# An mLSTM and pooling block on one core: decay rows behind the first queries, squares on VectorE, later casts, stores on SyncE

## The chip, the core and the metric

The kernel runs on one core of a Trainium2 chip. A core has TensorE (matmuls), VectorE, ScalarE and GpSimd (elementwise work), SyncE (it issues DMAs), and 16 DMA engines. The metric is the device time of one execution in microseconds (us), a median over runs. Time before: 2036.6 us, median of 3 runs (2034.02 to 2039.65).

## The reference

All values are float32. A latent stream x of 1024 tokens x 1024 channels passes two layers; 256 context tokens are read by the first. Each layer does `x = x + gate * rmsnorm(mixer(modulate(rmsnorm(x))))`, with shift, scale and gate from `silu(c) @ w_ada + b_ada`.

```
def rmsnorm(x, g):
    y = x * rsqrt(mean(x * x, axis=-1) + EPS)
    return y * g
```

- Layer A mixes with a bidirectional mLSTM of 4 heads of 512. Features of 2048 channels come from `h @ w_in`, a convolution over 3 tokens and SiLU; q, k and v are small block products of them. Per head the output is a product of masked, exponentially decayed scores with the values: `num = (q k^T * exp(d - m)) v`, divided by `max(|sum of weights|, exp(-m))`, and a normalisation over the head follows. Gates (sigmoid, SiLU) and `@ w_out` end it.
- Layer B mixes with box means of 4 sizes over the 16 x 64 grid: `u, z = split(h @ w_in)`, `y = (mean(u) - u) @ w_pool`, then `(y * silu(z)) @ w_out`.

The squares `x * x` of the post norm's and the next pre norm's sums are one part of what is changed; the casts of the values v, the order of the first head's loads and the stores of `x + ...` are the others.

## The kernel before

Channels lie on the 128 partitions, tokens in the free dimension, in chunks of 512, 512 and 256 (`CHUNKS`). A float32 product is three matmuls in a reduced format, hi x hi, hi x lo and lo x hi (`mm3`, L136 is the matmul). For weights `load_w` does a DMA on SyncE (L140), a copy on ScalarE for hi (L142) and a difference on VectorE for lo (L144), in two buffers each (`wr`, `wh`, `wl`), or five (`T5`) in the last stage.

The stages, in order of time:

- Start: condition vectors, norms (to about 91 us).
- Features, n = 0 to 15 (to about 363 us): products with `w_in` (evictions L373, L375), convolution (L378 to L381), and `token_part` (L395) for ten token tiles of 128: two matmuls each into a PSUM tile `pb` (two buffers), an eviction on ScalarE (L415) into a tile `vst` of five token tiles, after five tiles an addition of its halves on VectorE (L416), then the cast to hi on ScalarE (L418), lo on VectorE (L419) and two stores (L421).
- z and output gates (to about 671 us), with SiLU and sigmoid on ScalarE (L610, L615) and products on VectorE (L593, L616).
- Heads (from about 672 to 1192 us), 4 heads x 8 query tiles. A head needs its x features (`fetch_x`: L685, L691), decay rows (`load_gates`, L712; `load_ctx_gates`, L705), a block matrix A (`make_A`, L721 casts it), and queries (`make_q`, evicted on ScalarE L734 and VectorE L735). A query tile has scores in three PSUM tiles `pa` (three buffers in all), multiplied by decay weights on VectorE (L754); these weights are exponentials on ScalarE (`decay`, L768 to L772). Values (`fetch_v`, L699) are multiplied later. Pieces of the condition's product with `w_ada` are loaded meanwhile (L668) and added on VectorE (L670, L672).
- Output product with `w_out` for two halves of 512 tokens (`product`), each with squares (`squares`: first on ScalarE L979, others L982 on ScalarE, then an addition into `acc`, L983), a sum of the squares over the partitions by matmuls (`rstd_rows`), the residual (`residual`: L1002, L1003, store L1007), squares of that, and the next layer's input (`next_input`). `norm0` is spread as background work between the matmuls of the following product. Residuals run on VectorE and GpSimd in the first half, on VectorE in the second (`R0`).
- Layer B (to the end), with the same `product` and `residual` for `bw_out`, in pieces of 512, 256 and 256 tokens; its residuals run on GpSimd (`R1`), and a last one behind everything.

The order of TensorE's instructions is written by hand, except in the head phase. There, and on all other engines, a scheduler with a simulated timeline decides it, on the condition of the program's dependences and the ring buffers (`tl`: each tag has so many buffers, and a new tile waits until the one so many before is free). An engine runs its instructions in that order, so one that waits holds all behind it; SyncE's queue holds nearly all loads, GpSimd's the stores.

Of the kernel before, what the change touches and what calls it, by code (L numbers as in the profile page):

```python
# [12 lines left out]
F32R = mybir.dt.float32r  # L13
AF = mybir.ActivationFunctionType
ALU = mybir.AluOpType
AX = mybir.AxisListType

P = 128
# [33 lines left out]
def hybrid_block(ctx: ExitStack, tc: tile.TileContext, xT, ctxT, vecs, w_ada0, w_ada, w_blk, w_krow, blk_mask, w_gate, w_in, b_gate, w_out,  # L52
                 bw_in, bw_pool, bw_out, inv_cnt, outT):
    nc = tc.nc
    V, S, G, PE = nc.vector, nc.scalar, nc.gpsimd, nc.tensor
# [7 lines left out]
    def nm(s):  # L63
        uid[0] += 1
        return f"{s}_{uid[0]}"
# [11 lines left out]
    def tl(tag, shape, dt=F32):  # L77
        n = int(np.prod(shape[1:])) * 4
        assert n <= BYTES[tag], (tag, shape)
        pool = ph["pool"] if tag in PHASED else sb  # L80
        return pool.tile(list(shape), dt, tag=tag, bufs=BUFS[tag], name=nm(tag))
# [3 lines left out]
    def pt_(tag, shape=(P, 512)):  # L85
        return ps.tile(list(shape), F32, tag=tag, bufs=PBUFS[tag], name=nm(tag))
# [4 lines left out]
    def f(t):  # L91
        return t.bitcast(F32)
# [4 lines left out]
    def small1(shape, tag, bufs=2, dt=F32):  # L97
        return ph["pool"].tile(list(shape), dt, tag=tag, bufs=bufs, name=nm(tag))
# [25 lines left out]
    vh_d = dr.tile([NH, P, 10, DH], F32, name="vh_d")  # L124
    vl_d = dr.tile([NH, P, 10, DH], F32, name="vl_d")
# [9 lines left out]
    def mm(out, lhsT, rhs, start, stop):  # L135
        PE.matmul(out, lhsT, rhs, start=start, stop=stop)  # L136
# [76 lines left out]
    for kind in LOADS:  # L213
        if kind == "x":
            t = tl("S4", [P, T])
            nc.sync.dma_start(t, xT[:, len(x_sb)])
            x_sb.append(t)
        elif kind == "c":
            t = tl("S4", [P, 4, TC])
# [4 lines left out]
    acc = tl("wh", [P, T])  # L224
    for k in range(KD):
        if k == 0:
            S.activation(acc, x_sb[k], AF.Square)
        else:
            sq = tl("S4", [P, T])
            S.activation(sq, x_sb[k], AF.Square)  # L230
            V.tensor_tensor(acc, acc, sq, op=ALU.add)
    sq = [tl("S4", [P, 4, TC]) for _ in range(2)]
    for k in range(2):
# [15 lines left out]
                    op=ALU.add)  # L249
# [145 lines left out]
    def token_part(n, xmh, xml, xch, xcl):  # L395

        bv = small1([P, 32, 4], "bv", 1)
        V.tensor_tensor(bv, mask, wb[:, 2, n:n + 1].to_broadcast([P, 32, 4]), op=ALU.mult)
        bv = bv.rearrange("p a b -> p (a b)")
        vv = small1([P, 2, 144], "vv", dt=F32R)  # L400
        V.tensor_copy(vv[:, 0, :P], bv)
        V.tensor_tensor(vv[:, 1, :P], bv, f(vv[:, 0, :P]), op=ALU.subtract)
        V.tensor_copy(vv[:, :, P:], f(gm_all[:, n]).rearrange("p (a b) -> p a b", a=2))
        for s0 in (0, 5):
            vst, vhl = tl("T5", [P, 2, 5, 144]), tl("T5", [P, 2, 5, P], F32R)
            for s in range(s0, s0 + 5):
                yield
                if s < 8:
                    ah, al = xmh[0][:, s * P:(s + 1) * P], xml[0][:, s * P:(s + 1) * P]
                else:  # L410
                    ah, al = xmh[1][:, (s - 8) * P:(s - 7) * P], xml[1][:, (s - 8) * P:(s - 7) * P]
                p = pt_("pb", [P, 2, 144])
                mm(p.rearrange("p a b -> p (a b)"), ah, vv.rearrange("p a b -> p (a b)"), True, False)
                mm(p[:, 0], al, vv[:, 0], False, True)
                S.activation(vst[:, :, s - s0], p, AF.Copy)  # L415
            V.tensor_tensor(vst[:, 0], vst[:, 0], vst[:, 1], op=ALU.add)  # L416
            V.tensor_tensor(pre[:, s0:s0 + 5], pre[:, s0:s0 + 5], vst[:, 0, :, P:], op=ALU.add)
            S.activation(vhl[:, 0], vst[:, 0, :, :P], AF.Copy)  # L418
            V.tensor_tensor(vhl[:, 1], vst[:, 0, :, :P], f(vhl[:, 0]), op=ALU.subtract)  # L419
            for t, dst in ((vhl[:, 0], vh_d), (vhl[:, 1], vl_d)):  # L420
                nc.gpsimd.dma_start(dst[n // 4, :, s0:s0 + 5, (n % 4) * P:(n % 4 + 1) * P], f(t))  # L421
        yield

        gx = gx_all[:, n]
        for ci, (o, w) in enumerate(CHUNKS):
            ch, cl = (xch[0][:, o:o + w], xcl[0][:, o:o + w]) if ci < 2 else (xch[1], xcl[1])
            if n == 0:
                mm(gacc[ci][:32, :w], gx, ch, True, False)
                mm(gacc[ci][:16, :w], gx[:, :16], cl, False, False)
            else:  # L430
                mm(gacc[ci][:16, :w], gx[:, :16], cl, False, False)
                mm(gacc[ci][:32, :w], gx, ch, False, n == KE - 1)
# [262 lines left out]
    def fetch_v(hd, h, j0, j1):  # L695
        for j in range(j0, j1):
            for part, src in (("vh", vh_d), ("vl", vl_d)):
                t = tl("S4", [P, 2, DH], F32R)
                nc.sync.dma_start(f(t), src[h, :, 2 * j:2 * j + 2])  # L699
                hd.setdefault(part, []).append(t)  # L700

    def load_ctx_gates(h):
        rc = tl("hn" if h else "S4", [P, 2, TC])
        for d in range(2):
            nc.sync.dma_start(rc[:, d], a_d[32 * d + h:32 * d + h + 1, T:TA].to_broadcast([P, TC]))  # L705
        return rc

    def load_gates(h):
        out = []
        for d in range(2):  # L710
            r = tl("S4", [P, T])
            nc.sync.dma_start(r, a_d[32 * d + h:32 * d + h + 1, 0:T].to_broadcast([P, T]))  # L712
            out.append(r)
        return out

    def make_A(h):
        ah, al = tl("wh", [P, 4, 32, 4], F32R), tl("wl", [P, 4, 32, 4], F32R)
        r = tl("wr", [P, 4, 32, 4])
        for c in range(4):
            V.tensor_tensor(r[:, c], mask, amat[:, 4 * h + c:4 * h + c + 1].to_broadcast([P, 32, 4]), op=ALU.mult)  # L720
        V.tensor_copy(ah, r)  # L721
        V.tensor_tensor(al, r, f(ah), op=ALU.subtract)
        return ah.rearrange("p c a b -> p c (a b)"), al.rearrange("p c a b -> p c (a b)")

    def make_q(hd, A, tp):
        qh, ql = tl("S4", [P, 4, 256], F32R), tl("S4", [P, 4, 256], F32R)
        for c2 in range(2):
            p = pt_("pc", [P, 2, 256])
            for j in range(2):
                c = 2 * c2 + j  # L730
                o = tp % 2 * 256
                mm3(p[:, j], A[0][:, c], A[1][:, c], hd["xh"][c, tp // 2][:, o:o + 256],
                    hd["xl"][c, tp // 2][:, o:o + 256], True, True)
            S.activation(qh[:, 2 * c2:2 * c2 + 2], p, AF.Copy)  # L734
            V.tensor_tensor(ql[:, 2 * c2:2 * c2 + 2], p, f(qh[:, 2 * c2:2 * c2 + 2]), op=ALU.subtract)  # L735
        return qh, ql
# [100 lines left out]
    def start_head(h):  # L837
        hd = {}
        fetch_x(hd, h, 0)
        return dict(h=h, hd=hd)  # L840

    def next_q(cur, tp):
        return make_q(cur["hd"], cur["A"], tp)

    def finish_x(cur):
        for ci in (1, 2):
            fetch_x(cur["hd"], cur["h"], ci)

    cur = start_head(0)
    cur["R"], cur["rc"] = load_gates(0), load_ctx_gates(0)  # L850
    finish_x(cur)
    cur["A"] = make_A(0)
    cur["q"] = next_q(cur, 0)
    fetch_v(cur["hd"], 0, 0, 5)
    st_prev = st_now = nxt = None
    for i in range(len(seq) + 1):
# [42 lines left out]
        if st and ti == 7:  # L899
            cur = nxt  # L900
# [76 lines left out]
    def squares(src, acc, n, w):  # L977
        if n == 0:
            S.activation(acc, src, AF.Square)  # L979
        else:  # L980
            sq = tl("pt", [P, w])
            S.activation(sq, src, AF.Square)  # L982
            G.tensor_tensor(acc, acc, sq, op=ALU.add)  # L983

    def fetch_res(xsrc, o, w, tag):
        out = []
# [7 lines left out]
    def residual(yo, rs, o, w, xr, dst, acc2, engs):  # L994
        per = 1024 // w
        if engs[0] is G:
            rss = tl("hn", [P, w])
            S.activation(rss, rs, AF.Copy)
            rs = rss
        for n in range(8):  # L1000
            t = yo[n // per][:, n % per]
            engs[0].tensor_tensor(t, t, rs, op=ALU.mult)  # L1002
            engs[1].tensor_tensor(t, t, xr[n // per][:, n % per], op=ALU.add)  # L1003
            if acc2 is not None:
                squares(t, acc2, n, w)
            if n % per == per - 1:
                nc.gpsimd.dma_start(dst[:, n - per + 1:n + 1, o:o + w], yo[n // per])  # L1007
            yield STEP_R * w / 512

    gg0 = const([P, 8], "gg0")  # L1010
# [20 lines left out]
    def norm0(yo, acc, hf, tag):  # L1031
        xr = fetch_res(xT, 512 * hf, 512, tag)
        yield 4
        rs = yield from rstd_rows([acc], 512)
        acc2 = tl("hn", [P, 512])
        yield from residual(yo, rs, 512 * hf, 512, xr, x1_d, acc2, R0[hf])
        yield W2[hf]
        rs = yield from rstd_rows([acc2], 512)
        yield from next_input(yo, rs, hf)
# [5 lines left out]
    for hf in range(2):  # L1045
# [4 lines left out]
        yo, acc = [], tl("hn", [P, 512])  # L1050
# [130 lines left out]
    for hf in range(2):  # L1181
# [5 lines left out]
        for o, w in ((0, 512),) if hf == 0 else ((0, 256), (256, 256)):  # L1187
            yo, acc = [], tl("hn", [P, w])
# [11 lines left out]
    for e, i, n0, n1 in ((V, 0, 0, 4), (G, 1, 2, 4), (V, 1, 0, 2)):  # L1200
        t = yo[i][:, n0:n1]
# [84 lines left out]
```

## Time and profile before

| | before |
|---|---|
| median of 3 runs | 2036.6 us |
| profiled execution, span in the trace | 2035.27 us, 2032.8 us |
| mean granted TensorE clock | 0.992 of full speed |
| TensorE busy | 1970.0 us (97%) |
| VectorE busy | 1256.6 us (62%) |
| ScalarE busy | 812.5 us (40%) |
| GpSimd busy | 500.2 us (25%) |

Busy time counts instructions that compute; a TensorE that is busy may run at a lower granted clock, which stands in a column of its own. Where an engine idles, a row names after `<-` the engine, tile and line whose end released it. The lines of the rows are those of the kernel before; in the changed kernel the same code stands 8 to 10 lines lower.

### The profile page before, as it was taken

What the parts mean: (1) busy time and instruction counts of PE and PEld (TensorE: products, weight loads), DVE (VectorE), ACT (ScalarE), POOL (GpSimd) and SP (SyncE); (2) the same over time, 40 slices, a digit from 0 to 9 for tenths busy, and PEclk for the clock granted to TensorE, in tenths of its full rate; (3) what the DMA queues carried; (4) which work ended last, traced back from release to release, by engine and by line L of the source; (5) the groups of instructions that cost most, each with busy time, mean ns of one, the idle gap of its engine ahead of it and who ended that gap; (6) DMA issues with size and microseconds to landing.
All of it is one profiled execution on the core that took longest, in us unless ns stands there. A gap on an engine that the chain in (4) does not pass through costs nothing.

```text
span 2032.8 us, 26908 instructions
## 1 busy us (share of the span) xinstructions
PE 1970.0 (97%) x10050; PEld 1661.2 (82%) x10050; DVE 1256.6 (62%) x2092; ACT 812.5 (40%) x1357; POOL 500.2 (25%) x682
## 2 busy tenths in 40 slices
PE   6899999999999899999999999999999999999997
PEld 4788888788888688888888878887888888888897
DVE  4777777777767567676576662544747292744444
ACT  5567777433333433323332232533423131224443
POOL 2144334354443111111111101524000000000285
PEclk9999999999999999999999999999999999999998
DMA  9377777854444746446363324534331312133473
GB/s 360 130 259 256 257 258 253 319 167 135 131 150 132 295 148 210 179 140 242 111 232 126 133 70 153 196 113 166 94 114 42 104 52 92 49 114 140 166 272 122
DMA packets 115986, 339.47 MB, mean 167 GB/s; under 512 B 13036, under 2 KB 20716, under 8 KB 115856
## 3 DMA queue, kind: packets, MB, share of 16 engines
q1 hardware_dynamic: 85824, 234.80, 34.2%
q0 software_dynamic: 30032, 102.96, 13.7%
q8 instruction: 78, 1.28, 0.3%
q14 instruction: 52, 0.43, 0.1%
HBM read 234.77 MB, written 102.94 MB: 166 GB/s over the span
## 4 chain that ended last, share of the span: by engine, by line
PE 89%; DMA 3%; ACT 3%; DVE 2%; POOL 2%; issue 1%; SPq 0%; POOLq 0%; DVEq 0%; ACTq 0%
PE pa L136 45%; PE pc L136 34%; PE pb L136 7%; PE pb L795 2%; POOL hn L983 1%; PE pc L826 1%; DVE S L915 1%; DMA S<-in_w_ada_dram 1%; DMA S<-in_ctxT_dram 0%; DMA cst<-in_w_blk_dram 0%; DMA S<-a_d 0%; DMA wr<-in_w_ada_dram 0%; DMA S<-in_xT_dram 0%; POOL S L1003 0%; ACT wh L142 0%
## 5 line engine op out<-in xcount | busy, mean ns | idle before, releaser
L136 PE MATMUL pa<-S,wh 128*128 128x512 f32 (+1 forms) x2448 | 703.5, 372 | 0.0
L136 PEld LDWEIGHTS pa<-S,wh 128*128 128x128 f32 x2448 | 433.9, 189 | 67.7
L136 PE MATMUL pc<-S,wh 128*128 128x512 f32 (+1 forms) x1664 | 465.3, 366 | 1.8 <-DVE wh L721 0.9
L136 PE MATMUL pa<-S,wl 128*128 128x512 f32 (+1 forms) x1224 | 449.9, 368 | 0.1
L136 PEld LDWEIGHTS pc<-S,wh 128*128 128x128 f32 x1664 | 301.3, 189 | 53.4 <-DVE S L915 1.5
L144 DVE TENSOR_TENSOR wl<-wr,wh 128x1024 fp32r<-128x1024 f32 (+1 forms) x124 | 150.2, 1211 | 264.4 <-ACT wh L142 263.2
L136 PE MATMUL pc<-S,wl 128*128 128x512 f32 (+1 forms) x832 | 302.6, 365 | 0.3 <-DVE wl L144 0.2
L142 ACT ACTIVATE wh<-wr 128x1024 fp32r<-128x1024 f32 (+1 forms) x124 | 124.7, 1006 | 365.1 <-PE pc L136 144.4
L136 PEld LDWEIGHTS pa<-S,wl 128*128 128x128 f32 x1224 | 230.5, 188 | 39.8 <-DVE wl L144 0.5
L136 PE MATMUL pa<-S,S 128*128 128x512 f32 (+1 forms) x1152 | 249.6, 363 | 8.0 <-ACT S L734 8.0
L136 PE MATMUL pc<-S,pt 128*128 128x512 f32 x960 | 227.6, 392 | 0.8 <-DVE pt L798 0.5
L136 PEld LDWEIGHTS pa<-S,S 128*128 128x128 f32 x1152 | 192.3, 190 | 37.3 <-ACT S L734 8.6
L136 PEld LDWEIGHTS pc<-S,pt 128*128 128x128 f32 x960 | 178.3, 188 | 37.8 <-DVE S L735 1.0
L136 PEld LDWEIGHTS pc<-S,wl 128*128 128x128 f32 x832 | 157.4, 189 | 26.0 <-DVE wl L144 0.8
L983 POOL TENSOR_TENSOR hn<-hn,pt 128x512 f32<-128x512 f32 (+1 forms) x48 | 75.7, 1578 | 284.4 <-ACT pt L982 283.5
L797 ACT ACTIVATE pt<-pb 128x512 fp32r<-128x512 f32 (+1 forms) x96 | 47.8, 524 | 221.6 <-PE pb L795 221.6
L754 DVE SCALAR_TENSOR_TENSOR T<-pa,T 128x256 f32<-128x256 f32 (+3 forms) x184 | 78.2, 455 | 32.7 <-PE pa L136 31.8
L584 ACT ACTIVATE wh<-T 128x512 fp32r<-128x512 f32 x70 | 41.2, 627 | 96.3 <-PE pc L136 79.5
L136 PE MATMUL pb<-S,wh 128*128 128x512 f32 x256 | 78.9, 389 | 0.0
L415 ACT ACTIVATE T<-pb 128x288 f32<-128x288 f32 x160 | 62.5, 413 | 40.5 <-PE pb L136 33.0
L808 DVE BATCH_NORM_STATS2 st<-pc 128x6 f32<-128x512 f32 x32 | 22.4, 699 | 86.6 <-PE pc L136 86.5
L144 DVE TENSOR_TENSOR wl<-T,wh 128x1024 fp32r<-128x1024 f32 x32 | 45.7, 1428 | 43.4 <-ACT wh L142 43.3
(344 smaller groups left out, 2591.5 us busy)
## 6 DMA issues: line engine op xcount, KB each, us to landing
wr<-in_bw_in_dram SPq DMA_DIRECT2D x40, 512.0 KB, 3.6
wr<-in_w_in_dram SPq DMA_DIRECT2D x34, 512.0 KB, 4.2
wr<-in_w_ada_dram SPq DMA_DIRECT2D x32, 512.0 KB, 4.2
wr<-in_w_out_dram SPq DMA_DIRECT2D x32, 512.0 KB, 3.6
T<-in_bw_out_dram SPq DMA_DIRECT2D x32, 512.0 KB, 4.0
S<-y_d SPq DMA_DIRECT2D x28, 512.0 KB, 7.4
vh_d<-T POOLq DMA_DIRECT2D x32, 320.0 KB, 4.7
vl_d<-T POOLq DMA_DIRECT2D x32, 320.0 KB, 4.5
```

The costliest lines, as they stand in the source:

```text
L136: PE.matmul(out, lhsT, rhs, start=start, stop=stop)
L142: S.activation(h, r, AF.Copy)
L144: V.tensor_tensor(l, r, f(h), op=ALU.subtract)
L415: S.activation(vst[:, :, s - s0], p, AF.Copy)
L584: S.activation(hi, a, AF.Copy)
L754: V.scalar_tensor_tensor(W[:, lo + sh:hi + sh], p[:, lo - o:hi - o], 1.0, W[:, lo + sh:hi + sh], op0=ALU.mult, op1=ALU.mult, accum_out=dp[ ...
L795: PE.transpose(p[:, j], st["M"][:, s * P:(s + 1) * P], ident)
L797: S.activation(th[:, :n], p[:, :n], AF.Copy)
L808: V.bn_stats(b6, pv)
L826: PE.transpose(p[:, c], hn[:, c * P:(c + 1) * P], ident)
L915: V.tensor_tensor(b, yraw[kp, hf], f(a), op=ALU.subtract)
L983: G.tensor_tensor(acc, acc, sq, op=ALU.add)
```

## The change

Four edits:

1. In `token_part` the cast of a half's values becomes a function. It is called for the first half ahead of token tile 7, that is two tiles after the half's additions, and for the second half behind the last `yield`.
2. For head 0 the loads of the decay rows and of the context's decay rows stand behind the x loads, `make_A` and the first queries.
3. In `squares` the addition is VectorE's: 48 additions, 35 of 128x512 and 13 of 128x256.
4. The residual's stores are issued by SyncE: eight to x_d, six to the output.

```
+        def cast(s0, vst):
+            vhl = tl("T5", [P, 2, 5, P], F32R)
+            S.activation(vhl[:, 0], vst[:, 0, :, :P], AF.Copy)
+            V.tensor_tensor(vhl[:, 1], vst[:, 0, :, :P], f(vhl[:, 0]), op=ALU.subtract)
+            for t, dst in ((vhl[:, 0], vh_d), (vhl[:, 1], vl_d)):
+                nc.gpsimd.dma_start(dst[n // 4, :, s0:s0 + 5, (n % 4) * P:(n % 4 + 1) * P], f(t))
+
+        late = None
         for s0 in (0, 5):
-            vst, vhl = tl("T5", [P, 2, 5, 144]), tl("T5", [P, 2, 5, P], F32R)
+            vst = tl("T5", [P, 2, 5, 144])
             for s in range(s0, s0 + 5):
                 yield
+                if s == 7:
+                    cast(*late)
...
             V.tensor_tensor(pre[:, s0:s0 + 5], pre[:, s0:s0 + 5], vst[:, 0, :, P:], op=ALU.add)
-            S.activation(vhl[:, 0], vst[:, 0, :, :P], AF.Copy)
-            V.tensor_tensor(vhl[:, 1], vst[:, 0, :, :P], f(vhl[:, 0]), op=ALU.subtract)
-            for t, dst in ((vhl[:, 0], vh_d), (vhl[:, 1], vl_d)):
-                nc.gpsimd.dma_start(dst[n // 4, :, s0:s0 + 5, (n % 4) * P:(n % 4 + 1) * P], f(t))
+            late = s0, vst
         yield
+        cast(*late)
...
     cur = start_head(0)
-    cur["R"], cur["rc"] = load_gates(0), load_ctx_gates(0)
     finish_x(cur)
     cur["A"] = make_A(0)
     cur["q"] = next_q(cur, 0)
+    cur["R"], cur["rc"] = load_gates(0), load_ctx_gates(0)
     fetch_v(cur["hd"], 0, 0, 5)
...
             S.activation(sq, src, AF.Square)
-            G.tensor_tensor(acc, acc, sq, op=ALU.add)
+            V.tensor_tensor(acc, acc, sq, op=ALU.add)
...
             if n % per == per - 1:
-                nc.gpsimd.dma_start(dst[:, n - per + 1:n + 1, o:o + w], yo[n // per])
+                nc.sync.dma_start(dst[:, n - per + 1:n + 1, o:o + w], yo[n // per])
```

How the order on an engine changes is shown at three places. The first is ScalarE in the features, at the place that the trace of before has at 144.6 to 148.7 us: L373 and L375 evict feature chunks, L415 (L425 after) token tiles, L418 (L406 after) is the cast. ScalarE before:

```order
L375 ACTIVATE S_212_1239<-pa_1241 128x512
L373 ACTIVATE T_210_1234<-pa_1289 128x512
L375 ACTIVATE S_212_1239<-pa_1289 128x512
L418 ACTIVATE T_218_1255<-T_217_1254 128x640
L415 ACTIVATE T_225_1316<-pb_1324 128x2x144
L415 ACTIVATE T_225_1316<-pb_1334 128x2x144
```

ScalarE after the change, from the same place on:

```order
L375 ACTIVATE S_212_1239<-pa_1241 128x512
L425 ACTIVATE T_224_1311<-pb_1318 128x2x144
L373 ACTIVATE T_210_1234<-pa_1288 128x512
L375 ACTIVATE S_212_1239<-pa_1288 128x512
L425 ACTIVATE T_224_1311<-pb_1328 128x2x144
L406 ACTIVATE T_228_1342<-T_217_1254 128x640
L425 ACTIVATE T_224_1311<-pb_1347 128x2x144
```

One token eviction now stands between the first two feature evictions, and a second one ahead of the cast.

The second is SyncE at the start of the heads. L691 and L685 (L699, L693) load x features, L712 and L705 (L720, L713) decay rows, L820 (L828) gate rows, L668 (L676) pieces of w_ada, L699 (L707) values. SyncE before:

```order
L691 DMA S_1051_6137<-xl_d 128x2x512
L691 DMA S_1052_6139<-xl_d 128x2x512
L712 DMA S_1053_6141<-a_d 128x1024
L712 DMA S_1054_6143<-a_d 128x1024
L705 DMA S_1055_6145<-a_d 128x256 x2
L691 DMA S_1056_6148<-xh_d 128x2x512
L691 DMA S_1057_6150<-xh_d 128x2x512
```

SyncE after the change, from the gate rows on, some nine rows further down:

```order
L828 DMA ab_6380<-gb_d 128x512
L828 DMA ab_6525<-ga_d 128x512
L676 DMA wr_6569<-in_w_ada_dram 128x1024
L676 DMA wr_6572<-in_w_ada_dram 128x1024
L720 DMA S_1066_6182<-a_d 128x1024
L720 DMA S_1067_6184<-a_d 128x1024
L713 DMA S_1068_6186<-a_d 128x256 x2
L707 DMA S_1069_6189<-vh_d 128x1024
L707 DMA S_1070_6191<-vl_d 128x1024
```

The decay rows stand behind the x rows, the gate rows and two pieces of w_ada, directly ahead of the values.

The third is VectorE at the end of the output product's second half. L1003 (L1011) adds residuals, L144 splits weights, L947 is the first step behind the sum of the squares, L991 (after only) adds squares. VectorE before:

```order
L1003 TENSOR_TENSOR S_2227_12544<-S_2227_12544,S_2247_12636 128x512
L144 TENSOR_TENSOR wl_12789<-wr_12785,wh_12787 128x1024
L1003 TENSOR_TENSOR S_2227_12544<-S_2227_12544,S_2247_12636 128x512
L144 TENSOR_TENSOR wl_12834<-wr_12830,wh_12832 128x1024
L144 TENSOR_TENSOR wl_12886<-wr_12882,wh_12884 128x1024
L947 TENSOR_SCALAR r_2284_12854<-pb_12849 128x4
```

VectorE after the change, from the same place on:

```order
L1011 TENSOR_TENSOR S_2227_12544<-S_2227_12544,S_2247_12636 128x512
L144 TENSOR_TENSOR wl_12789<-wr_12785,wh_12787 128x1024
L1011 TENSOR_TENSOR S_2227_12544<-S_2227_12544,S_2247_12636 128x512
L991 TENSOR_TENSOR hn_12689<-hn_12689,pt_12704 128x512
L144 TENSOR_TENSOR wl_12834<-wr_12830,wh_12832 128x1024
L991 TENSOR_TENSOR hn_12689<-hn_12689,pt_12719 128x512
L991 TENSOR_TENSOR hn_12689<-hn_12689,pt_12746 128x512
L991 TENSOR_TENSOR hn_12689<-hn_12689,pt_12761 128x512
L991 TENSOR_TENSOR hn_12689<-hn_12689,pt_12775 128x512
L991 TENSOR_TENSOR hn_12689<-hn_12689,pt_12803 128x512
L144 TENSOR_TENSOR wl_12886<-wr_12882,wh_12884 128x1024
L991 TENSOR_TENSOR hn_12689<-hn_12689,pt_12817 128x512
```

Seven additions have come in: the first ahead of one split, five ahead of the next, the last behind it.

## Rows read from the trace of the kernel before

**Rows 1.** The page, part 4: shares of the chain that ended last.

```profile
PE 89%; DMA 3%; ACT 3%; DVE 2%; POOL 2%; issue 1%; SPq 0%; POOLq 0%; DVEq 0%; ACTq 0%
```

**Rows 2.** Waits of TensorE: us in total, times, longest us.

```profile
PE pb L136 <- ACT T L415: 10.8, 9, 2.4
PE pa L136 <- ACT S L734: 8.0, 2, 7.8
PE pb L136 <- POOL hn L983: 6.5, 3, 4.8
...
PE pc L136 <- DVE wh L721: 0.9, 1, 0.9
```

**Rows 3.** Windows, TensorE: us, busy (instructions), granted clock, DMA share, GB/s.

```profile
80.00:113.00 33.00, 27.64 (x148) 1.00 0.53 183
...
683.00:690.00 7.00, 6.88 (x26) 0.69 1.03 408
700.00:1180.00 480.00, 479.50 (x2595) 1.00 0.48 165
...
1418.00:1426.00 8.00, 7.88 (x29) 0.59 0.00 0
```

**Rows 4.** Waits of TensorE from 96 to 113, and from 113 to 355 us.

```profile
PE pb L136 <- ACT T L415: 2.9, 3, 1.8
...
PE pb L136 <- ACT T L415: 4.6, 4, 1.1
```

**Rows 5.** Timeline, ScalarE near 147 us: start us, us, instruction.

```profile
147.08 0.74 ACT L418 ACTIVATE T<-T 128x640 fp32r<-128x640 f32 x1
```

**Rows 6.** Timeline, SyncE at the first head.

```profile
658.55 1.01 SPq L712 DMA_DIRECT2D S<-a_d  x2
...
673.97 1.42 SPq L668 DMA_DIRECT2D wr<-in_w_ada_dram  x2
```

**Rows 7.** Timeline at the first head: ScalarE, VectorE, TensorE.

```profile
666.97 1.28 ACT L769 ACT_TABLE_LOAD   x1 [3.17 <-DMA S<-a_d]
...
682.49 1.55 ACT L734 ACTIVATE S<-pc 128x512 fp32r<-128x512 f32 x3
...
671.23 0.75 DVE L616 SCALAR_TENSOR_TENSOR hn<-hn,vec,S 128x512 f32<-128x512 f32 x1 [3.91 <-ACT hn L615]
...
683.12 6.83 PE L136 MATMUL pa<-S,S 128*128 128x512 f32 x24 [7.85 <-ACT S L734]
```

**Rows 8.** DMA issues from 650 to 700 us: size, median us to landing.

```profile
S<-a_d SPq DMA_DIRECT2D x2, 512.0 KB, 9.3
```

**Rows 9.** Timeline of the output product: TensorE, GpSimd, VectorE.

```profile
1328.92 1.05 PE L136 MATMUL pb<-ones,hn 128*128 128x1 f32 x8 [1.29 <-POOL hn L983]
...
1411.88 6.19 POOL L983 TENSOR_TENSOR hn<-hn,pt 128x512 f32<-128x512 f32 x4
...
1418.12 1.86 PE L136 MATMUL pb<-ones,hn 128*128 128x1 f32 x8 [4.84 <-POOL hn L983]
...
1312.89 4.39 DVE L144 TENSOR_TENSOR wl<-wr,wh 128x1024 fp32r<-128x1024 f32 x1 [3.78 <-ACT wh L142]
...
1399.77 4.30 DVE L1003 TENSOR_TENSOR S<-S,S 128x512 f32<-128x512 f32 x7
1403.98 1.23 DVE L144 TENSOR_TENSOR wl<-wr,wh 128x1024 fp32r<-128x1024 f32 x1
...
1411.47 2.81 DVE L144 TENSOR_TENSOR wl<-wr,wh 128x1024 fp32r<-128x1024 f32 x1 [3.41 <-ACT wh L142]
```

**Rows 10.** Timeline, last stage: GpSimd, SyncE, ScalarE.

```profile
1954.69 7.03 POOL L1003 TENSOR_TENSOR S<-S,S 128x512 f32<-128x512 f32 x4
...
1954.53 2.20 SPq L990 DMA_DIRECT2D S<-x_d  x4
...
1968.56 1.06 ACT L142 ACTIVATE wh<-T 128x1024 fp32r<-128x1024 f32 x1 [1.18 <-PE pa L136]
```

**Rows 11.** The page, part 6: KB each, median us to landing.

```profile
T<-in_bw_out_dram SPq DMA_DIRECT2D x32, 512.0 KB, 4.0
```

## Prediction

> **What bounds the kernel now.** I read the chain that ended last first: TensorE is 89% of it [rows 1]. The reader should then ask where TensorE does *not* work, since only there can time come back. In the head phase from 700 to 1180 us it idles for half a microsecond in 480 [rows 3]: nothing can be gained there. The list of TensorE's waits gives the places: 10.8 us behind evictions L415 of the feature phase, 8.0 us behind the eviction L734 of the first queries, 6.5 us behind the square additions L983 on GpSimd [rows 2]. That is 25.3 us, and three of the edits touch exactly these lines. The windows add a second loss: after a long gap the granted clock drops. Behind the gap that ends at 683 us it is 0.69 on average for 7 us, with TensorE busy in nearly all of them; behind the one that ends at 1418 us it is 0.59 for 8 us; but over 80 to 113 us, where the gaps are 1 to 3 us long, it stays at 1.00 [rows 3]. So a long gap costs itself and 0.31 x 7 = 2.2 us, or 0.41 x 8 = 3.3 us, after it.
>
> **The change part by part.** All sums are made against the profiled execution, 2035.27 us (span 2032.8), which is 1.3 us under the median of 2036.6.
>
> *Casts two tiles later.* Each feature evicts ten token tiles from two PSUM buffers on ScalarE. Before, the cast L418 of the first five stood ahead of the eviction of the sixth. At 147 us the row shows it: the cast runs at 147.08 for 0.74 us [rows 5], only then come two evictions, and TensorE, whose next tile needs one of these buffers, waits 1.1 us. Four places are alike between 113 and 355 us, 4.6 us together, and three between 96 and 113 us make 2.9 us [rows 4]. After the change the order puts one eviction between those of the feature's chunks (L375, L373) and the second ahead of the cast, so that both buffers are free when TensorE comes. No instruction is added: the same casts, VectorE differences and stores, only later. The first half's tile is held two token tiles longer in its ring of five and its stores leave later; the next tile in the same place of the ring is most of a feature away, so I cost this at nothing; without that cover evictions would wait for stores in place of casts, and the gain would be the lower bound, 0. Of 7.5 us I take 6.5, since at one of the three early places other ScalarE work stands in the way too. Bounds: 0 (another instruction takes the cast's place) and -10.8 (all waits on L415).
>
> *First head.* Before, SyncE issued the two decay rows at 658.55 us, ahead of half of the x rows [rows 6]. On ScalarE the scheduler put the exponentials, which wait for these rows, ahead of the query evictions: a table load has waited until 666.97, a chain of exponentials with three more table loads follows, and L734 comes at 682.49, though the queries had left TensorE at 683.12 - 7.85 = 675.3 [rows 7]. TensorE idles these 7.85 us. The same queue held L615, on which VectorE waited 3.9 us until 671.23 (L616), and with it the cast L721 that the queries needed, 0.9 us [rows 2, 7]. With the clock's 2.2 us, about 11 us are lost here.
> After the change SyncE issues the row transfers behind the w_ada pieces, which in the profile went out at 673.97 [rows 6] because they wait for VectorE steps that L616 delayed; they should now go 1 to 2 us earlier, so the rows leave at about 673 to 675.5. Landing took 9.3 us in the median between 650 and 700 us with the DMA queues full [rows 8], but now all x rows stand ahead of them and are gone by then; I take 5 to 7 us, an estimate between nothing queued and that median. The exponentials then start at 679 to 682, and the first scores can be multiplied by their weights 2 to 3 us after. Meanwhile TensorE has 42 matmuls: the scores of the first tile fill the three "pa" buffers, and the next queries follow. At the mean of 700 to 1180 us (480 / 2595 = 0.185 us each) they last 7.8 us, so TensorE runs from about 674.5 to 682.5 and then waits 0 to 3 us for a buffer. Left over: 1 us for the evictions and 2 us for this wait, at full clock, since gaps of this size kept it in rows 3. So -8; bounds -11 (everything) and +3 (the rows need 9.3 us from 676, exponentials and table loads take until 690, and TensorE waits 7 us there with the clock loss behind it and finds the value rows late as well).
>
> *Squares on VectorE.* On GpSimd they end late twice. After the first half's residual TensorE has waited 1.29 us at 1328.92; in the second half four additions in a row take 6.19 us from 1411.88, TensorE waits 4.84 us and then loses 3.3 us to the clock [rows 3, 9]. With the third wait, the whole is 6.5 + 3.3 = 9.8 us. On VectorE the nearest row is the 128x512 sum of two SBUF tiles L1003: 4.30 us for seven, 0.61 each [rows 9]. In the second half the order has five additions behind a weight split L144, one more split and the last addition; that split starts at 1411.47 behind ScalarE's and takes 1.23 us undisturbed (1403.98), the last addition 0.6: the sum is ready at 1413.3, and TensorE, done at 1418.12 - 4.84 = 1413.28, waits next to nothing beyond a hand-over of some tenths. In the first half VectorE idles 3.78 us ahead of 1312.89 [rows 9], where five additions fit, 14 us ahead of TensorE. I take -8.5; bounds -9.8 and 0.
> What is new on VectorE is 48 x 0.61 = at most 29 us, in stages where VectorE idles for some 3.4 us ahead of a split (1411.47 in rows 9), so an addition fits between. This cover is gone if GpSimd slows VectorE. The row that warns is L144 at 1312.89: 4.39 us, while GpSimd added residuals [rows 9]. The Trainium skill ("SBUF — State Buffer", section "Who interferes with whom") says that a VectorE instruction with two SBUF inputs and a GpSimd instruction that reads SBUF hold one another off for their whole length. The trace agrees in that place, and by the rule each addition could wait for one of GpSimd's, which speaks against this edit. In rows alone: a residual addition on GpSimd takes up to 7.03 / 4 = 1.76 us [rows 10], so seven additions held by one each last 7 x (0.61 + 1.76) = 16.6 us, from 1307 to 1324 in the first half, still ahead of 1327.6; and 48 additions leave GpSimd, so the splits meet fewer. I keep the sum.
>
> *Residual stores on SyncE.* They leave GpSimd and join SyncE's queue, where a store that waits for its additions holds every weight load behind it. In the first layer's halves the next load waits for a weight split anyway, so the store costs nothing. The narrow place is the last stage: the fourth output store waits for GpSimd's additions that end at 1961.7, or about 1960 without the square between them; behind it stand four x_d loads, which took 2.2 us from 1954.53, and the next weight load, which would leave at 1962.5. With 4.0 us of landing [rows 11] it is there at 1966.5, behind the x_d data at the latest at 1968; ScalarE splits it at 1968.56 [rows 10]. So 0, with 0 to 2 us to spare; bounds 0 and +6 (3 us late, and a clock loss of 3 us).
>
> **Sum.** -6.5 - 8 - 8.5 + 0 = -23.0, so 2012.3 for an execution like the profiled one, 2013.6 from the median.
>
> **Rivals.**
> 1. *The first head's wait only moves.* For: the windows have DMA at 408 GB/s there [rows 3], the rows now queue behind w_ada pieces, and VectorE's w_ada step stands ahead of the first masked product. Against: the x rows are gone earlier. The wait for "pa" is then 5 to 8 us, this part gives -1 to -3, in all 2019 to 2021.
> 2. *VectorE becomes late.* Additions held by GpSimd push back L144, and each late split costs TensorE 1 to 2 us at four or five product blocks. For: 4.39 us at 1312.89. Against: the additions that leave GpSimd. The squares then give -2, in all 2020.
> 3. *The casts' edit does nothing*: another ScalarE instruction ends last at the same places. Tokens give -1, in all 2019.
> 4. *SyncE's queue blocks (slower).* Stores that wait for residual additions hold weight loads by more than the prefetch covers. It decides from the point where the store due at 1960 goes out later than 1963: every load of the next stage is then late with it. At three such places (both halves of the first layer, the last stage) a stall of 5 us with a clock loss of 3 us each gives 24, and the splits' lateness that follows takes the 8.5 of the squares: 32.5 against 23 gained, 2045. For: three loads of the last stage are mixed with the stores. Against: the lead of the ring of five, and that the first layer's loads wait for splits anyway.
>
> **How the numbers follow.** My forecast has 0.6, rival 1 0.14, rival 2 0.09, rival 3 0.08, rival 4 0.04, and 0.05 is for mixtures of the first three that leave almost nothing. The range is from 2006 (all bounds together, -10.8 - 11 - 9.8 = -31.6, would give 2005) to 2026 (two rivals at once). A difference under 0.3%, 6 us, could not be told from none here. Faster by more (under 2030.5): 0.87; the same: 0.09; slower (over 2042.7): 0.04.
>
> **What would show it.** In the changed profile: no wait on the token eviction at every third feature; the first query evictions ahead of any table load, scores from about 674 and the granted clock at 1.00 after; no wait over 1 us ahead of the sums of squares, no half clock there; no TensorE wait on a weight split in the last stage. It is wrong if a wait for decay weights of over 5 us stands at 682, if L144 on VectorE is waited for in the output products, or if weight loads show up in TensorE's waits of the last stage.

## The result and the profile after

| | before | after |
|---|---|---|
| median of 4 runs | 2035.31 us (2032.28 to 2039.65) | 2020.29 us (2018.48 to 2022.27) |
| profiled execution, span | 2035.27 us, 2032.8 us | 2018.94 us, 2017.2 us |
| TensorE busy | 1970.0 us | 1970.4 us |
| VectorE, ScalarE, GpSimd busy | 1256.6, 812.5, 500.2 us | 1287.7, 807.1, 419.6 us |
| mean granted clock | 0.992 | 0.992 |

The ratio is 0.9925 with an interval of 0.9902 to 0.9947: 15 us faster, where 23 were forecast; the range held the time. Measured again beside the experiments below, the changed kernel gave 0.9924 (0.9909 to 0.9938).

Lines of the changed kernel are 8 to 10 higher than those of the kernel before. TensorE's waits in it (us in total, times, longest) stand against [rows 2]:

```profile
PE pa L136 <- DVE T L762: 4.3, 1, 4.3
PE pb L136 <- ACT T L425: 4.1, 4, 2.4
...
PE pc L136 <- ACT wh L142: 2.2, 1, 2.2
...
PE pc L136 <- DVE wl L144: 0.7, 2, 0.5
...
PE pb L136 <- DVE hn L991: 0.2, 1, 0.2
```

The 10.8, 8.0 and 6.5 us have become 4.1 (2.4 of them at 91 us and 1.1 at 354 us), nothing, and 0.2. New are 4.3 us on the masked products of the first head (L762), and 2.2 + 0.5 us on a weight that is split late in the last stage. The windows give the granted clock (us, busy, granted clock, DMA share, GB/s), against [rows 3]:

```profile
680.00:683.00 3.00, 3.00 (x9) 0.50 1.02 418
1385.00:1400.00 15.00, 14.96 (x66) 1.00 0.61 217
1953.00:1956.00 3.00, 2.48 (x10) 0.52 0.97 391
1956.00:1960.00 4.00, 4.00 (x22) 0.51 0.66 245
```

The output product's second half runs through at full clock. At half the clock are now 680 to 683 us, behind the wait of the first head, and 1953 to 1960 us, in the last stage. So is a part of 92 to 104 us (the last row of this document), where the kernel before had the same gap and kept 1.00.

Outside the head phase the order of TensorE's 10050 matmuls is the same but for eight of them, so the two traces can be compared between the same matmuls. By the times of the kernel before, the changed one gains 0.7 us up to 91 us, 5.5 in the features (91 to 361), 5.3 in the heads (671 to 1200), 9.5 at the sums of squares (1325 to 1430), and loses 6.2 in the last stage (1950 to 1985). The stretches between change by 0.4 us or less, and 14.8 us are gained at 2015.

**Features.** The waits between 96 and 355 us, 2.9 + 4.6 us before [rows 4], and ScalarE at the first of the four alike places:

```profile
PE pb L136 <- ACT T L425: 0.5, 2, 0.3
```

```profile
144.33 0.59 ACT L375 ACTIVATE S<-pa 128x512 fp32r<-128x512 f32 x1
144.81 0.41 ACT L425 ACTIVATE T<-pb 128x288 f32<-128x288 f32 x1
...
146.84 0.42 ACT L425 ACTIVATE T<-pb 128x288 f32<-128x288 f32 x1
```

Evictions L425 now stand between and right behind those of the features; the cast comes after them. The waits shrink by 7.0 us, and the stretch from 91 to 361 us by 5.5: in this execution the low clock between 92 and 104 us takes a part back. In two executions that kept 1.00 there (`e1_casts`, `e7_xd_pool` below) the same stretch is 8.4 and 8.3 us shorter.

**First head.** SyncE, ScalarE, VectorE and TensorE, against [rows 6, 7]:

```profile
663.98 3.01 SPq L676 DMA_DIRECT2D wr<-in_w_ada_dram  x2
667.15 0.86 SPq L720 DMA_DIRECT2D S<-a_d  x2
```

```profile
667.48 1.08 ACT L742 ACTIVATE S<-pc 128x512 fp32r<-128x512 f32 x2
...
671.64 1.28 ACT L777 ACT_TABLE_LOAD   x1
676.07 0.99 ACT L777 ACTIVATE T<-S,cst 128x128 f32<-128x128 f32 x3 [3.14 <-DMA S<-a_d]
```

```profile
676.87 0.29 DVE L762 SCALAR_TENSOR_TENSOR T<-pa,T 128x128 f32<-128x128 f32 x1 [0.22 <-POOL T L781]
...
678.57 0.69 DVE L762 SCALAR_TENSOR_TENSOR T<-pa,T 128x512 f32<-128x512 f32 x1 [1.40 <-ACT T L779]
```

```profile
667.22 3.06 PE L136 MATMUL pa<-S,S 128*128 128x512 f32 x13
...
679.33 10.63 PE L136 MATMUL pa<-S,S 128*128 128x512 f32 x44 [4.26 <-DVE T L762]
```

And the DMA issues from 650 to 700 us (KB, median us to landing), against [rows 8]:

```profile
S<-a_d SPq DMA_DIRECT2D x2, 512.0 KB, 9.3
```

The queries are evicted at once, scores start at 667.22. The decay rows are issued at 667.15, and L777 starts at 676.07, when the first of them has landed, 8.9 us later; the median of the two is 9.3 us, as it was in the kernel before. TensorE runs out of "pa" buffers at 679.33 - 4.26 = 675.07 and waits until the second masked product (678.57 for 0.69 us) frees one. Here the table load costs nothing, since it ends at 672.92 and the row is waited for until 676.07.

**Squares.** VectorE in both halves and GpSimd in the first, against [rows 9]:

```profile
1299.29 5.99 DVE L991 TENSOR_TENSOR hn<-hn,pt 128x512 f32<-128x512 f32 x4
...
1308.86 0.68 DVE L991 TENSOR_TENSOR hn<-hn,pt 128x512 f32<-128x512 f32 x1
```

```profile
1298.38 5.55 POOL L1011 TENSOR_TENSOR S<-S,T 128x512 f32<-128x512 f32 x3
```

```profile
1394.63 3.66 DVE L991 TENSOR_TENSOR hn<-hn,pt 128x512 f32<-128x512 f32 x5
1398.62 1.23 DVE L144 TENSOR_TENSOR wl<-wr,wh 128x1024 fp32r<-128x1024 f32 x1 [0.34 <-ACT wh L142]
1399.77 0.68 DVE L991 TENSOR_TENSOR hn<-hn,pt 128x512 f32<-128x512 f32 x1
```

In the second half five additions take 3.66 us, then come the split and the last addition, and TensorE waits 0.2 us for them, within some tenths of the forecast. In the first half four additions take 5.99 us, 1.5 each where the second half has 0.7, while three residual additions of GpSimd take 5.55 us, 1.85 each where the five before them took 1.35. The Trainium skill ("SBUF — State Buffer", section "Who interferes with whom") states that a VectorE instruction with two SBUF inputs contends with a GpSimd instruction that reads SBUF. The trace agrees: both are additions of two SBUF tiles, and once GpSimd is done, at 1303.9, VectorE's are back at 0.7 us. That the overlap is the cause is not shown by a run of its own. It costs nothing here: the last addition ends at 1309.5, and TensorE comes to the sum at 1316.4.

**Last stage.** SyncE, ScalarE and TensorE, against [rows 10, 11], and the landing of the one weight load that is issued at 1943.63 (KB, us), followed by that of the same load in the kernel before, issued at 1957.09:

```profile
1940.41 0.40 SPq L1015 DMA_DIRECT2D out_dram<-S  x1
1940.89 2.64 SPq L998 DMA_DIRECT2D S<-x_d  x4
1943.63 28.12 SPq L140 DMA_DIRECT2D T<-in_bw_out_dram  x11
```

```profile
1944.98 1.06 ACT L142 ACTIVATE wh<-T 128x1024 fp32r<-128x1024 f32 x1 [1.82 <-PE pc L136]
...
1951.92 1.06 ACT L142 ACTIVATE wh<-T 128x1024 fp32r<-128x1024 f32 x1 [5.25 <-DMA T<-in_bw_out_dram]
```

```profile
1953.03 0.77 PE L136 MATMUL pc<-S,wh 128*128 128x256 f32 x2 [2.21 <-ACT wh L142]
```

```profile
T<-in_bw_out_dram SPq DMA_DIRECT2D x1, 512.0 KB, 8.2
...
T<-in_bw_out_dram SPq DMA_DIRECT2D x1, 512.0 KB, 9.7
```

The fourth output store waits for GpSimd until 1940.41, four x_d loads follow, and the next weight load goes out at 1943.63. It would be split at about 1947.9 (one split each 2.9 us: 1944.98, then this one), but it has landed only 8.2 us after its issue, and is split at 1951.92. TensorE waits 2.21 us, 0.5 us more for VectorE's part, and then runs 7 us at half clock: 2.7 + 3.4 = 6.1 us. The landing is not longer than it was: in the kernel before, with the stores on GpSimd, the same load took 9.7 us, but it went out 11.5 us ahead of its split (1968.56 in [rows 10]). What the stores on SyncE take away is this lead.

### The profile page after: what moved, and what is told of

It is laid out like the page before. It is cut to its first block, busy times and chain, and to the rows that moved or that the text cites. A ratio compares the mean times of both kernels' runs of the same rounds, so it can differ in the third digit from the quotient of the medians.

```text
span 2017.2 us, 26878 instructions
## 1 busy us (share of the span) xinstructions
PE 1970.4 (98%) x10050; PEld 1662.4 (82%) x10050; DVE 1287.7 (64%) x2140; ACT 807.1 (40%) x1353; POOL 419.6 (21%) x620
## 4 chain that ended last, share of the span: by engine, by line
PE 90%; DMA 3%; DVE 3%; ACT 2%; issue 1%; POOL 1%; SPq 0%; POOLq 0%; DVEq 0%; ACTq 0%
PE pa L136 46%; PE pc L136 35%; PE pb L136 7%; PE pb L803 2%; DVE S L923 1%; PE pc L834 1%; DMA S<-in_w_ada_dram 1%; DVE wl L144 1%; DMA S<-in_ctxT_dram 1%; DMA S<-a_d 0%; POOL S L1011 0%; DMA wr<-in_w_ada_dram 0%; DMA T<-in_bw_out_dram 0%; DMA cst<-in_w_blk_dram 0%; ACT wh L142 0%
## 5 line engine op out<-in xcount | busy, mean ns | idle before, releaser
L144 DVE TENSOR_TENSOR wl<-wr,wh 128x1024 fp32r<-128x1024 f32 (+1 forms) x124 | 144.1, 1162 | 249.3 <-ACT wh L142 248.0
L762 DVE SCALAR_TENSOR_TENSOR T<-pa,T 128x256 f32<-128x256 f32 (+3 forms) x184 | 78.3, 453 | 33.4 <-PE pa L136 27.2
L957 POOL TENSOR_TENSOR r4b<-r,mhalf 128x4 f32<-128x4 f32 (+1 forms) x7 | 9.2, 1320 | 389.4 <-DVE r L955 389.4
L425 ACT ACTIVATE T<-pb 128x288 f32<-128x288 f32 x160 | 63.0, 416 | 42.3 <-PE pb L136 31.9
L144 DVE TENSOR_TENSOR wl<-T,wh 128x1024 fp32r<-128x1024 f32 x32 | 45.5, 1423 | 37.6 <-ACT wh L142 37.6
```

Of the source, the lines that this page charges most:

```text
L144: V.tensor_tensor(l, r, f(h), op=ALU.subtract)
L762: V.scalar_tensor_tensor(W[:, lo + sh:hi + sh], p[:, lo - o:hi - o], 1.0, W[:, lo + sh:hi + sh], op0=ALU.mult, op1=ALU.mult, accum_out=dp[ ...
L957: G.tensor_tensor(r2[:, :nb], r[:, :nb], mhalf[:, :nb], op=ALU.pow)
```

## The experiments

Results are ratios to the kernel before, run on the same chip beside each group of experiments. Its median was 2039.1 us beside the four edits alone, 2036.3 beside the next four runs, and 2036.7 beside the last two. The gains in us are worked out from these.

**Each edit alone.** Of the change's diff only one part was made each time: the cast (edit 1), the order of the first head's loads (edit 2), `V.tensor_tensor(acc, acc, sq, op=ALU.add)` (edit 3), `nc.sync.dma_start(...)` for the residual's stores (edit 4).

```
 e1_casts:   + if s == 7: cast(*late)  ...  + cast(*late)
 e2_head:    + cur["R"], cur["rc"] = load_gates(0), load_ctx_gates(0)    (behind next_q)
 e3_squares: - G.tensor_tensor(acc, acc, sq, op=ALU.add)
             + V.tensor_tensor(acc, acc, sq, op=ALU.add)
 e4_stores:  - nc.gpsimd.dma_start(dst[:, n - per + 1:n + 1, o:o + w], yo[n // per])
             + nc.sync.dma_start(dst[:, n - per + 1:n + 1, o:o + w], yo[n // per])
```

> Only the casts are moved; the rest is as before. If the casts were what stood in front of the token evictions, the four waits near every third feature (4.6 us) and the three before 113 us (2.9 us) go, the features end 5 to 6.5 us earlier than before, and the time is 2029 to 2030 against 2035.3 before. Rival: the gain of the features needs nothing else but is lost again before the heads (the z and output gates then wait for something later); then the features end earlier and the time is unchanged, 2034 to 2036.

Measured: 0.9943 (0.9930 to 0.9955), 11.6 us. The waits between 96 and 355 us fell from 7.5 to 1.7 us, of which 1.1 us is a wait that lies behind 355 us in the kernel before; the theory holds. More was gained than the waits amount to. Between the same matmuls of the two traces the features are 8.4 us shorter, 2.1 us are gained before 91 us, ahead of anything that the edit touches, and 1.0 lost after. So 8.4 us are shown to come from the features; the rest is within what executions of one kernel differ by.

> Only the first head's decay rows are loaded behind its queries. Theory: the wait is exchanged, 7.8 us on the query eviction for about 4.3 us on the first masked product (rows not landed), with a shorter stretch of low clock; 5 to 6 us are gained, 2029 to 2030. Rival: the 4.3 us come from the other edits (earlier arrival of TensorE); alone the wait is under 2 us and 8 us are gained, 2027.

Measured: 0.9962 (0.9948 to 0.9975), 7.7 us, with an interval of 5.1 to 10.6 that holds both forecasts. The trace decides: the wait is there without the other edits, and longer:

```profile
PE pa L136 <- DVE T L754: 5.1, 1, 5.1
```

So the theory's mechanism stands: the wait was exchanged for a shorter one. Between the same matmuls the heads of this trace gain 3.5 us, less than either sum.

> Only the squares are added on VectorE; the stores stay on GpSimd. Theory: the waits before the sums of squares (1.3 and 4.8 us) and the low clock behind the second go, 9 us gained, 2026. Rival: with the stores still issued by GpSimd the residual additions on GpSimd end later and VectorE's additions are held; then 4 to 6 us are gained, 2029 to 2031, and a wait of over 1 us stands before a sum of squares.

Measured: 0.9955 (0.9942 to 0.9967), 9.2 us. Of the waits ahead of a sum of squares 0.4 us is left, and between the same matmuls 1325 to 1430 us is 9.2 us shorter. The rival falls.

> Only the residual stores are issued by SyncE; squares stay on GpSimd. Theory: in the last stage the stores hold the weight loads; GpSimd's squares put the fourth store 1.7 us later still, so TensorE waits 3 to 5 us for a weight and then runs at low clock, 6 to 9 us lost, 2041 to 2044. Rival: the wait in the changed kernel comes from the whole being earlier (DMA busier in that stretch), not from the stores; alone they cost nothing, 2034 to 2036.

Measured: 1.0008 (0.9999 to 1.0017), no loss that can be told from none, though the trace has the wait of the theory:

```profile
PE pb L136 <- POOL hn L983: 4.0, 2, 3.6
...
PE pc L136 <- ACT wh L142: 2.5, 1, 2.5
```

Both theories missed something. TensorE waits 2.5 us for a weight in the last stage, but GpSimd, rid of the issue of the stores (0.7 us each), ends its squares earlier: 4.0 us of waits in place of 6.5 [rows 2]. Between the same matmuls the last stage loses 6.3 us and the sums of squares gain 2.4. With the squares on VectorE this second effect has nothing left to give, and the loss stands alone. Edits 3 and 4 share a gain.

**The last stage: who holds the weight?** Two kernels start from the changed one.

```
 e6_out_back: - nc.sync.dma_start(dst[:, n - per + 1:n + 1, o:o + w], yo[n // per])
              + (nc.gpsimd if dst is outT else nc.sync).dma_start(...)
 e7_xd_pool:  - xr = fetch_res(x1_d, o, w, "S4")
              + xr = fetch_res(x1_d, o, w, "S4", nc.gpsimd if w == 256 else nc.sync)
              - xr = fetch_res(x1_d, 768, 256, "S4")
              + xr = fetch_res(x1_d, 768, 256, "S4", nc.gpsimd)
```

> The changed kernel itself, unaltered, as the yardstick of the next three. All theories: the time against before as first measured, ratio 0.990 to 0.995; in the trace the wait of 2.2 us for a weight split in the last stage and 4.3 us for the first masked product again, while the clock behind the 2.4 us gap at 91 us may or may not be low, since equal gaps in other runs showed both.

Measured: 0.9924 (0.9909 to 0.9938), with waits of 2.7 us for the weight and 4.5 us for the masked product.

> As the changed kernel, but the six output stores of the last stage are issued by GpSimd again; the x_d stores stay on SyncE. Theory: only these stores hold the weight loads, so the wait in the last stage (2.2 + 0.5 us) and the low clock behind it (3.4 us) go, 5 to 6 us faster than the changed kernel, ratio to before 0.988 to 0.990. Rival: the loads are late because DMA is full there (x_d rows and weights), whoever issues the stores; then a wait of 2 us stays and under 2 us are gained.

Measured: 0.9894 (0.9879 to 0.9909), 6.1 us less than the changed kernel beside it; in the traces the last stage gives 5.2 of it. SyncE, ScalarE, and the landing of the same weight load:

```profile
1934.19 2.28 SPq L998 DMA_DIRECT2D S<-x_d  x4
1936.58 27.48 SPq L140 DMA_DIRECT2D T<-in_bw_out_dram  x10
```

```profile
1948.33 1.06 ACT L142 ACTIVATE wh<-T 128x1024 fp32r<-128x1024 f32 x1 [1.18 <-PE pa L136]
```

```profile
T<-in_bw_out_dram SPq DMA_DIRECT2D x1, 512.0 KB, 10.0
```

The same weight load goes out at 1936.58, 7 us earlier. It takes 10.0 us to land, and is still split when its turn comes, at 1948.33. So it was the place in SyncE's queue that made it late.

> As the changed kernel, but the four x_d loads of the last stage are issued by GpSimd in place of SyncE, behind its additions, so that the weight load follows the fourth output store at once, some 2.7 us earlier. If the queue alone makes the weight late, the wait shrinks to under 0.5 us and 5 us are gained; if full DMA queues do (landing 8 us where 4 are usual), the x_d data compete as before, the landing stays near 7 us and a wait of 1 to 2 us with low clock stays.

Measured: 0.9900 (0.9884 to 0.9915), 4.9 us less than the changed kernel. GpSimd's x_d loads, SyncE's weight load and its landing:

```profile
1937.18 3.07 POOL L998 DMA_DIRECT2D S<-x_d  x4
```

```profile
1937.27 0.39 SPq L1015 DMA_DIRECT2D out_dram<-S  x1
1937.76 18.86 SPq L140 DMA_DIRECT2D T<-in_bw_out_dram  x9
```

```profile
T<-in_bw_out_dram SPq DMA_DIRECT2D x1, 512.0 KB, 6.9
```

The weight load follows the store at once, 2.7 us earlier than in the changed kernel (the whole stage is 3.1 us earlier here, so 1937.76 is 1940.9 there). Its lead over its split, at 1944.78, is 7.0 us where it was 4.3. Its landing is long, but 1.3 us shorter than in the changed kernel, and no wait of over 0.3 us for a weight is left. So this run alone does not part the two causes: with 8.2 us of landing a wait of about 1 us could have stayed. The run above does.

**The first head: rows earlier.** From the kernel with the output stores back, the row loads were put right behind the x rows:

```
     finish_x(cur)
+    cur["R"], cur["rc"] = load_gates(0), load_ctx_gates(0)
     cur["A"] = make_A(0)
     cur["q"] = next_q(cur, 0)
-    cur["R"], cur["rc"] = load_gates(0), load_ctx_gates(0)
```

> As the one with the output stores back on GpSimd, and the first head's decay rows loaded right behind the x rows, ahead of the gate rows and w_ada pieces, some 8 us earlier than in the changed kernel. If the 4.3 us wait on the first masked product is the landing of the rows behind w_ada, it goes with the low clock behind it: 5 to 6 us faster than the kernel it starts from, ratio to before 0.985 to 0.988. Rival: the exponentials then stand ahead of other ScalarE work again (the second queries' evictions), and TensorE waits for these; gain 0 to 2 us.

Measured: 0.9903 (0.9887 to 0.9919): the 5 to 6 us of the theory are not gained against 0.9894; a small gain cannot be told, with intervals that reach 3 us to either side. TensorE, and VectorE ahead of its new wait:

```profile
684.20 8.34 PE L136 MATMUL pa<-S,S 128*128 128x512 f32 x41 [0.98 <-DVE T L762]
...
709.11 0.44 PE L803 MATMUL pb<-ident,T 128*128 128x128 f32 x2 [1.96 <-DVE pt L806]
```

```profile
703.42 1.28 DVE L680 SCALAR_TENSOR_TENSOR wl<-wr,csil,wl 128x1024 f32<-128x1024 f32 x1 [2.19 <-DMA wr<-in_w_ada_dram]
705.77 1.28 DVE L680 SCALAR_TENSOR_TENSOR wl<-wr,csil,wl 128x1024 f32<-128x1024 f32 x1 [1.07 <-DMA wr<-in_w_ada_dram]
...
708.38 0.68 DVE L806 TENSOR_TENSOR pt<-pb,pt 128x512 fp32r<-128x512 f32 x1
```

```profile
702.00:722.00 20.00, 16.25 (x74) 0.83 0.53 165
```

The longest wait on the masked product shrinks to 0.98 us, so it was the landing of the rows. (They went out at 659.24, 8 us earlier, but took 12.0 us to land: the first exponential starts at 672.12, 4 us earlier.) But VectorE is now at pieces of w_ada (L680) that have not landed, with L806 queued behind them, and TensorE waits 3.7 us for L806; the clock falls to 0.83 over 20 us. Neither theory had this place; the rival's sum was right by another cause.

Then the w_ada pieces of the first head were added one query tile later (`ADA_STEPS[ti - 1]` for head 0, none at tile 0):

> As the one with the early decay rows (right behind the x rows) and the output stores back on GpSimd, and the pieces of w_ada of the first head are added one query tile later (none at tile 1, one at tile 2, and so on to tile 6). If the 3.7 us wait near 709 us of that kernel, on a VectorE that stood at a w_ada piece whose load had not landed, ate the gain of the earlier decay rows, both waits are gone now, and the time is 5 us under the kernel with only the output stores back (ratio to before 0.986 to 0.988). Rival: the pieces stand in VectorE's way wherever they are put, the wait appears at a later tile, and the time stays within 2 us of it (0.989 to 0.991).

> The changed kernel with the output stores back on GpSimd once more, as the yardstick for the run beside it: ratio to before 0.988 to 0.991 by both theories, with the 4.2 us wait on the first masked product and no wait in the last stage.

Measured side by side: 0.9891 (0.9875 to 0.9907) with the earlier rows and later pieces, 0.9891 (0.9873 to 0.9908) with the output stores back alone; the 5 us that the theory forecast are not seen, a smaller gain cannot be told. In the first of them the pieces still stand ahead of the product that TensorE needs, for 2.0 us in three waits:

```profile
PE pb L803 <- DVE pt L806: 2.0, 3, 1.1
```

The rival holds: the order of VectorE has two of these pieces ahead of L806 again, at 703.2 and 705.4 us, though a later tile asks for them. What the first head would be worth without them stays open; leaving them out was not tried. Nothing tried here is faster than the changed kernel with its output stores on GpSimd, 0.9894 and 0.9891 in two groups of runs: 21.6 to 22.2 us under the kernel before and 6 under the changed one.

## Why the prediction was right, and where its sum failed

- **Casts, -6.5.** The waits fell from 7.5 to 0.5 us, by the mechanism described. That the trace's gain, 5.5 us, is near the forecast is in part luck: without the low clock at 92 to 104 us it is 8.3 to 8.4, more than the waits.
- **First head, -8.** Order, start of the scores (667.22; all is 6.2 us earlier by then, so 673.4 in the forecast's time) and the end of the buffers (681.3, forecast 682.5) came as written, and the 1 us for the evictions did not appear. Mis-sized was "I take 5 to 7 us" for the landing of the rows: it was 8.9 and in the median 9.3, the other end of the estimate. The x rows had been issued 9 us or more ahead of them, but DMA was as full as before (a share of 1.04 from 668 to 676 us). The wait is 4.26 us in place of 2, and "at full clock, since gaps of this size kept it" fell with it: 3 us at 0.50. So 5.3 us in the trace; four other traces with the same code for the heads have 2.5 to 5.6, and 3.5 in `e2_head`. Rival 1, that the wait only moves, was half true.
- **Squares, -8.5.** 9.2 us alone and 9.5 in the changed kernel's trace; waits and low clock are gone. VectorE was slowed beside GpSimd as rival 2 had it, but where it had time.
- **Stores, 0, bound +6.** This step failed, and in the trace by its full bound, 6.2 us; taking the six output stores back gave 6.1 us. "With 4.0 us of landing it is there at 1966.5" took the median of the whole program for this load, while the trace of the kernel before had 9.7 us for the load itself, and the changed one has 8.2. From 1962.5 that would have been 1972, 3.6 us behind the split at 1968.56: the upper bound, and not 0. The lead was also shorter than written, 4.3 us (1947.9 - 1943.6) and not 6.1 (1968.56 - 1962.5): GpSimd's additions ended about 1 us later than counted, and the store and the four x_d loads took SyncE longer. It is rival 4's place, at one of its three stages and with nothing lost before it, so that the price was 6 and not 32.
- **The sum.** Between the same matmuls, 5.5 + 5.3 + 9.5 - 6.2 = 14.1 us, with 0.7 us of scatter at the start 14.8; 15.0 were measured. The edits run alone add up to more (11.6 + 7.7 + 9.2 - 1.6 = 26.9 us). 2.5 us of that is the gain that edits 3 and 4 share. The four results also rest on one median of the kernel before, 2039.1 us, which is 2.4 to 3.8 us above its medians in the other groups, and such an error counts four times, about 10 to 15 us. This would explain the rest; it is not shown.

## What to carry to other kernels

Before a store that waits for computation joins a queue of loads, compare the lead of the loads behind it with the landing time *of those very loads* in the trace of before, not with the program's median: here it was 9.7 us where the median was 4.0. Where a wait on data is removed by reordering, the transfer itself has not become faster; see when its data lands and how long the work lasts that was moved ahead of it. Two edits that relieve the same engine may share one gain, so measure an edit in the company in which it will run. And to see what each edit gave inside one change, compare the times between the same matmuls of two traces, stage by stage; results of edits run alone, with intervals of 5 us, cannot be added up.

## What the runs showed of the hardware

The same gap near 91 us, 2.4 us of waiting, is in the traces of all twelve runs. The granted clock over 92 to 104 us in three of them, the kernel with the casts alone, the second run of the changed kernel, and its first:

```profile
92.00:104.00 12.00, 11.77 (x60) 1.00 0.74 262
```

```profile
92.00:104.00 12.00, 9.35 (x40) 0.86 0.47 175
```

```profile
92.00:104.00 12.00, 10.43 (x39) 0.72 0.48 163
```

It is 1.00, 0.86 and 0.72 for one and the same place. In seven of the twelve traces a part of this stretch is at 0.50, in five, that of the kernel before among them, none is; so [rows 3] could not show that gaps of this size keep the clock. By the end of the features the three differ by 0, 1.6 and 2.9 us. Executions of one kernel differ by some 10 us (before: 2030.5 to 2042.8 us), and their mean clock goes with the time (0.988 at 2041.5, 0.992 at 2033.8).
